# Weights laid out by the host as contiguous 1 MB blocks, 8 KB on each partition

## The chip, the core and the metric

The kernel runs on one core of a Trainium2 chip. The core has TensorE for matrix products, VectorE, ScalarE and GpSimd for elementwise work, and sixteen DMA engines that carry data from memory into the on-chip tiles of 128 partitions. The metric is the device time of one execution in microseconds.

## What is computed

The reference is a stack of two transformer blocks of the usual kind, followed by a third of another kind, on 256 tokens of 1024 features, in 32-bit floats:

```
x: [1, 256, 1024]
for layer in (0, 1):
    h = h + mixer(rmsnorm(h))                # layer 0: gated linear recurrence and forgetting attention
                                             # layer 1: dilated and sliding-window attention
    h = h + cross_attention(rmsnorm(h), mem) # q, k, v, o of 1024 x 1024 each
    h = h + relu(rmsnorm(h) @ w_up) ** 2 @ w_down          # 1024 -> 4096 -> 1024
h = rmsnorm(h)
mod = silu(c) @ w_ada + b_ada                # 1024 -> 6144: shifts, scales and gates
h = h + gt1 * hybrid_mixer(norm(h))          # attention and a gated delta rule, gated together
aff = softmax(h2 @ w_router)                 # 16 experts; each takes its 32 best tokens
y[e] = (silu(xe[e] @ w_gate[e]) * (xe[e] @ w_up[e])) @ w_down[e]     # each matrix 1024 x 1024
h = h + gt2 * (sum of gates * y, put back to the tokens)
```

Each weight is used once. Those of the experts are 3 x 16 x 1024 x 1024 floats, 201 MB of the 394 MB that the kernel reads.

## The kernel before

All weights come from memory in blocks of 1 MB into tiles of 128 partitions x 2048 floats, called `raw` (`fraw` for w_ada). The queue of SyncE issues nearly all of these loads, in the order of their use; a load waits until its tile has been used up by the work before.

The dense products of the first three quarters (`dense_fm_steps` L331, `dense_tm_steps` L353, `mlp` L583) are made with three products of 32-bit halves: `split` (L287) lets ScalarE write the upper part `whi` (L294) and VectorE the lower part `wlo` (L295) of 1024 columns at a time, and `mm3` (L310 to L313) lets TensorE multiply upper by upper, lower by upper and upper by lower. A block of `dense_fm` is 8 chunks of 128 rows by 256 columns of the matrix, so a partition gets 8 pieces of 256 floats (1 KB) from 8 rows; one of `dense_tm` and of the perceptrons' second matrix is 4 chunks by 512 columns (2 KB). `load_chunks` (L269) writes this as a rearranged view of the matrix. The vector `mod` is made beside the perceptrons by VectorE (`modulation`, L957), from blocks of 2 chunks by 1024 columns (4 KB) in tiles `fraw`. At the very start `mixer0` loads its input `xT` and its first weight block in three parts each, as `FIRST` says, so that the first product waits for a part only.

The experts run last. `experts` (L1798) takes them in four groups of 4, `G`. For each group the gate matrices are streamed (`stream`, L1784): for each chunk of 128 input features two blocks, each with 2 experts by 1024 columns (4 KB pieces), and 4 products on each block, in which two experts of 32 tokens stand side by side in the array (L1793). Then the up matrices in the same way, the activation, four transposes for each half, and the down matrices (L1825 to L1845): a block there has 4 experts by 512 columns (2 KB pieces; L1832 loads, L1835 multiplies). In the last group `TAIL` cuts the second half of the columns into two of 256: there a tile holds two chunks with two loads of 512 KB each (1 KB pieces). After a set of columns two products (L1842) put the rows back to their tokens, VectorE adds them to X (L1843), and in the last group the sum is written out (L1845).

Twenty tiles take the blocks of the experts in turn (`raw_tile`, L1773): 8 `early`, which the delta rule's systems use before, 4 `ring`, 5 `ring2` and 3 `ring3`, which come free as the mixer ends. The first blocks are loaded into them while the mixer and the routing still run.

The program's order on each engine is found by a scheduler, which simulates the instructions as they are written.

Of the kernel before, what the change touches and what calls it, by code (L numbers as in the profile page):

```python
# [15 lines left out]
PSUM = bass.MemoryType.PSUM  # L16

P = 128
# [54 lines left out]
def _kchunks(w):  # L73
    import numpy as np

    w = np.asarray(w)
    k, n = w.shape
    return w.reshape(k // P, P, n).transpose(1, 0, 2).reshape(P, -1)

# [131 lines left out]
class Chunks:  # L211
    """Feature chunks kept two to a tile, indexed as one [partition, chunk, token] array."""
# [14 lines left out]
def _body(ctx, tc, I, lay, out, stop):  # L227
# [46 lines left out]
    def wload(src, nk, n):  # L274
        raw = ring.tile([P, 2048], F32, name="raw")
        load_chunks(raw, src, nk)
        return raw

# [27 lines left out]
    def weights(src, nk, n, pre=None, part=1024, slow=()):  # L306
        raw = pre if pre is not None else wload(src, nk, n)
        return split(raw, nk, n, part, slow)
# [22 lines left out]
    def dense_fm_steps(W, c0, ncols, a, emit, kc=8, pre=None, slow=(), first=1024):  # L331
        ah, al = a
        for b0 in range(0, ncols, 256):
            wd = min(256, ncols - b0)
            nb = wd // P
            ws = weights(W[:, c0 + b0:c0 + b0 + wd], kc, wd, pre[b0 // 256] if pre else None, 1024 if b0 else first, slow)
# [16 lines left out]
    def dense_tm_steps(W, c0, ncols, a, emit, kc=8, step=512, part=1024):  # L353
        ah, al = a
        for g0 in range(c0, c0 + ncols, step):
            wd = min(step, c0 + ncols - g0)
            kt = 2048 // step
            ws = [weights(W[k0 * P:(k0 + kt) * P, g0:g0 + wd], kt, wd, part=part) for k0 in range(0, kc, kt)]
# [62 lines left out]
    def transpose_half(gain, j):  # L421
        # features first, for the products that come next: half of the features as soon as they are there
# [30 lines left out]
    def causal_pv(pool, es, v, vcols, o):  # L453
        # two heads at once: their columns of the array are separate
# [19 lines left out]
    def features_first(src, gain, pool, name, raw=None):  # L474
        if raw is None:
            raw = wload(src, 8, S)
# [18 lines left out]
    def mem_k(l, a, kT):  # L495
# [5 lines left out]
        return dense_fm_steps(I["xa_w_kv"][l], 0, D, a, ek)  # L501

    def mem_v(l, a, v):
# [3 lines left out]
        return dense_tm_steps(I["xa_w_kv"][l], D, D, a, ev, step=VS)  # L507

    def cross_attention(l, kT, v, pool):
# [12 lines left out]
        def split_own(x, nm, lo, w):  # L522
# [3 lines left out]
            for c in range(0, 2048, w):  # L526
# [8 lines left out]
               # the lower part of the values takes the place of the keys  # L535
               split_own(v, "vMh", lambda: kvs.tile([P, 2, D], F32R, name=f"kT{l}"), 512)]
        for n, _ in enumerate(dense_fm_steps(I["xa_w_q"][l], 0, D, a, eq)):
# [41 lines left out]
        dense_tm(I["xa_w_o"][l], 0, D, (oh, ol), add_x, gain=pv(f"g_ml{l}"))  # L579

    def mlp(l, pool, side, done):
# [4 lines left out]
        Wu, Wd = I["mlp_w_up"][l], I["mlp_w_down"][l]  # L586
# [26 lines left out]
        for g in range(8):  # L613
# [3 lines left out]
            for n in range(2):  # L617
                ws = weights(Wd[g * 512:(g + 1) * 512, n * 512:(n + 1) * 512], 4, 512)
# [15 lines left out]
    def mixer0(pool):  # L634
        W = I["ab_w_in"][0]
        # the first product waits for a half of its operands only
        xraw, wraw = (ring.tile([P, 2048], F32, name="raw") for _ in range(2))
        for k0, k1 in FIRST:
            load_chunks(xraw, I["xT"], 8, k0, k1)
            load_chunks(wraw, W[:, 0:256], 8, k0, k1)  # L640
        wraw = (wraw, wload(W[:, 256:512], 8, 256))
# [25 lines left out]
        # gated linear recurrence  # L667
# [10 lines left out]
        # forget gates: two copies of the eight rows  # L678
# [112 lines left out]
    def mixer1(pool):  # L791
        groups["k2"] = load_group(pool, "k2")
        W = I["cd_w_in"][0]
# [8 lines left out]
        # chunks: 0-3 qc, 4-7 kc, 8-11 qd, 12 kd, 13 kd with its two heads exchanged  # L802
# [98 lines left out]
    class Fill:  # L901
        # steps of other products, to stand between those of a chain
# [24 lines left out]
    def modulation(pool, units):  # L927
        # rows of silu(c) @ w_ada, 1024 columns to a unit: products by feature on DVE, the sum over the features by
        # TensorE at the end of each unit
        c = pv("c")  # L930
        cs = pool.tile([P, 8], F32, name="cs")
        # a window on these columns that starts at 96 - 32 q has ones in its columns 32 q to 32 q + 31 only
# [8 lines left out]
        def load(b, hf, k, first):  # L941
            raw = (ring if first else pool).tile([P, 2048], F32, name="raw" if first else "fraw")
            load_chunks(raw, I["w_ada_2"][0, k * P:(k + 2) * P, b * 2048 + hf * D:b * 2048 + (hf + 1) * D], 2)
            return raw

        for b, hf, k in [(b, hf, k) for b, hf in units for k in range(0, 8, 2)]:
            raw = load(b, hf, k, (b, hf, k) == (*units[0], 0))
# [1016 lines left out]
```

## Time and profile before

| | us |
|---|---|
| median of three runs | 1639.99 (1638.78 to 1642.88) |
| span of the profiled execution | 1637.7 |
| TensorE busy | 1462.6 (89% of the span) |
| VectorE busy | 871.8 (53%) |
| ScalarE busy | 610.1 (37%) |
| data read from memory | 393.62 MB, 241 GB/s over the span |

The profiled execution's own time is its span, 1637.7 us from the first to the last instruction; the median of the timed runs is 2.3 us above it. Busy time is what an engine's instructions cover, averaged over stages that differ. The DMA share of a stretch is the mean over the sixteen engines, and it goes a little over 1 where records of two transfers overlap. The clock of TensorE has two levels, 1.2 and 2.4 GHz, given as 0.50 and 1.00.

### The profile page before, as it was taken

How to read it: one execution, taken by the hardware profiler on the slowest of the kernel's cores; microseconds unless marked ns; L12 is line 12 of the kernel's file. 1: busy time of each engine (PE TensorE's matmuls, PEld its weight loads, DVE VectorE, ACT ScalarE, POOL GpSimd, SP SyncE). 2: the span in 40 equal slices, each digit the busy share in tenths (PEclk: the TensorE clock that was granted, in tenths of full speed). 3: DMA queues.
4: the chain of work that ended last, by engine and by line, in shares of the span. 5: the costliest groups of instructions: out<-in, count | busy, mean ns of one | idle time of the engine just before them, and what ended most of it. 6: DMA issues, size and time to landing. Idle time of an engine off the chain costs nothing.

```text
span 1637.7 us, 25415 instructions
## 1 busy us (share of the span) xinstructions
PE 1462.6 (89%) x10554; PEld 1076.7 (66%) x10554; DVE 871.8 (53%) x1556; ACT 610.1 (37%) x1005; POOL 98.8 (6%) x97
## 2 busy tenths in 40 slices
PE   8999999999999989999967999999797777777776
PEld 8978898999888788999956888899531111111111
DVE  7775668776666677876578985557521001001001
ACT  6755545444444665544435455425210000000000
POOL 0000200000000020000022512100000000000000
PEclk9989999999999999999988999999797996996996
DMA  8635547885543345976521412448699999999999
GB/s 305 207 105 189 170 129 265 288 298 192 179 145 136 104 155 183 315 277 234 195 85 52 130 53 74 161 159 290 243 403 399 411 403 402 414 408 395 413 406 310
DMA packets 212372, 396.33 MB, mean 242 GB/s; under 512 B 6880, under 2 KB 112352, under 8 KB 212128
## 3 DMA queue, kind: packets, MB, share of 16 engines
q1 hardware_dynamic: 211104, 391.27, 66.6%
q10 hardware_dynamic: 864, 2.64, 0.5%
q8 instruction: 83, 1.36, 0.3%
q0 software_dynamic: 288, 0.79, 0.1%
q14 instruction: 33, 0.27, 0.0%
HBM read 393.62 MB, written 1.05 MB: 241 GB/s over the span
## 4 chain that ended last, share of the span: by engine, by line
PE 63%; DMA 24%; DVE 8%; ACT 2%; issue 1%; SPq 1%; DVEq 0%; ACTq 0%
PE mm L313 13%; PE mm L312 13%; PE mm L311 13%; DMA raw<-in_w_down_dram 9%; DMA raw<-in_w_up_dram 8%; DMA raw<-in_w_gate_dram 5%; PE acc L312 3%; PE acc L313 3%; PE acc L311 3%; DVE wlo L295 2%; PE mm L1793 1%; PE acc L1450 1%; PE acc L1793 1%; DMA fraw<-in_w_ada_dram 1%; PE acc L464 1%
## 5 line engine op out<-in xcount | busy, mean ns | idle before, releaser
L295 DVE TENSOR_TENSOR wlo<-raw,whi 128x1024 fp32r<-128x1024 f32 (+1 forms) x303 | 369.3, 1223 | 179.4 <-ACT whi L294 172.7
L294 ACT CAST whi<-raw 128x1024 fp32r<-128x1024 f32 (+1 forms) x303 | 313.5, 1039 | 347.0 <-PE mm L312 176.5
L311 PE MATMUL mm<-hTh,whi 128*128 128x256 f32 x1096 | 312.7, 289 | 7.5 <-ACT whi L294 5.4
L313 PE MATMUL mm<-hTh,wlo 128*128 128x256 f32 x1096 | 313.4, 288 | 4.8 <-DVE wlo L295 4.8
L312 PE MATMUL mm<-hTl,whi 128*128 128x256 f32 x1096 | 314.3, 289 | 1.9 <-DVE hTl L1086 1.9
L311 PEld LDWEIGHTS mm<-hTh,whi 128*128 128x128 f32 x1096 | 211.2, 194 | 13.0 <-ACT whi L294 5.6
L313 PEld LDWEIGHTS mm<-hTh,wlo 128*128 128x128 f32 x1096 | 211.9, 194 | 8.9 <-DVE wlo L295 7.1
L312 PEld LDWEIGHTS mm<-hTl,whi 128*128 128x128 f32 x1096 | 211.9, 194 | 4.2 <-DVE hTl L1086 2.2
L1793 PE MATMUL mm<-raw,xe 128*32 128x512 f32 x512 | 108.2, 598 | 30.6 <-DMA raw<-in_w_up_dram 30.6
L1793 PE MATMUL acc<-raw,xe 128*32 128x512 f32 x512 | 102.4, 620 | 22.7 <-DMA raw<-in_w_gate_dram 22.7
L1793 PEld LDWEIGHTS mm<-raw,xe 128*32 128x32 f32 x512 | 22.3, 109 | 113.3 <-DMA raw<-in_w_up_dram 74.2
L1811 ACT ACTIVATE sgl<-acc 128x512 f32<-128x512 f32 x8 | 4.7, 597 | 230.1 <-PE acc L1793 230.1
L1793 PEld LDWEIGHTS acc<-raw,xe 128*32 128x32 f32 x512 | 21.6, 112 | 98.7 <-DMA raw<-in_w_gate_dram 57.1
L311 PE MATMUL acc<-whi,hh 128*128 128x512 f32 x192 | 75.0, 391 | 0.0
L312 PE MATMUL acc<-wlo,hh 128*128 128x512 f32 x192 | 74.9, 391 | 0.0
L313 PE MATMUL acc<-whi,hl 128*128 128x512 f32 x192 | 74.2, 390 | 0.0
L1820 DVE SCALAR_TENSOR_TENSOR sgl<-sgl,mm 128x512 f32<-128x512 f32 x8 | 5.4, 686 | 116.3 <-PE mm L1793 116.3
L1835 PE MATMUL acc<-raw,xe 128*32 128x512 f32 x256 | 47.7, 850 | 21.6 <-DMA raw<-in_w_down_dram 21.6
L1835 PE MATMUL mm<-raw,xe 128*32 128x512 f32 (+1 forms) x320 | 43.2, 641 | 26.0 <-DMA raw<-in_w_down_dram 26.0
L957 DVE SCALAR_TENSOR_TENSOR macc<-fraw,cs,macc 128x1024 f32<-128x1024 f32 x40 | 51.2, 1281 | 20.7 <-DMA fraw<-in_w_ada_dram 20.3
L1812 DVE SCALAR_TENSOR_TENSOR sgl<-sgl,acc 128x512 f32<-128x512 f32 x8 | 5.4, 686 | 106.3 <-ACT sgl L1811 106.3
L312 PE MATMUL mm<-wlo,hTh 128*128 128x256 f32 (+2 forms) x192 | 58.7, 307 | 0.3 <-DVE wlo L295 0.3
(525 smaller groups left out, 2618.2 us busy)
## 6 DMA issues: line engine op xcount, KB each, us to landing
raw<-in_w_gate_dram SPq DMA_DIRECT2D x64, 1024.0 KB, 17.8
raw<-in_w_up_dram SPq DMA_DIRECT2D x64, 1024.0 KB, 18.3
raw<-in_w_down_dram SPq DMA_DIRECT2D x56, 1024.0 KB, 14.4
raw<-in_mlp_w_up_dram SPq DMA_DIRECT2D x32, 1024.0 KB, 5.4
raw<-in_mlp_w_down_dram SPq DMA_DIRECT2D x32, 1024.0 KB, 5.4
fraw<-in_w_ada_dram SPq DMA_DIRECT2D x22, 1024.0 KB, 6.7
raw<-in_w_in_dram SPq DMA_DIRECT2D x19, 1024.0 KB, 5.1
raw<-in_xa_w_kv_dram SPq DMA_DIRECT2D x16, 1024.0 KB, 5.5
```

The lines of the kernel that those rows point to most:

```text
L294: nc.scalar.copy(hi[:, a:b], raw[:, c0 + a:c0 + b])
L295: (nc.gpsimd if len(parts) in slow else nc.vector).tensor_sub(lo[:, a:b], raw[:, c0 + a:c0 + b], f(hi[:, a:b]))
L311: mm(o, lh, rh, start=start, stop=False, skip_group_check=True)
L312: mm(o, lh, rl, start=False, stop=False, skip_group_check=True)
L313: mm(o, ll, rh, start=False, stop=stop, skip_group_check=True)
L464: mm(o[j * 64:j * 64 + 64, q0:S], v[:, k, vcol:vcol + 64], pT[:, c0:c0 + S - q0], start=k == 0, stop=k == 1, skip_group_check=True)
L957: nc.vector.scalar_tensor_tensor(acc[:, sl], w, ck, acc[:, sl], OP.mult, OP.add)
L1450: mm(o[J, c], lh[J, c], rh[J, c], start=True, stop=True)
L1793: ins = mm(banks[n][j * 32:(j + 1) * 32, :], xe[:, c, G * P + j * 32:G * P + (j + 1) * 32], raw[:, e * D + n * 512:e * D + (n + 1) * 512], ...
L1812: nc.vector.scalar_tensor_tensor(sg[:, sl], sg[:, sl], 1.0, bg[n], OP.add, OP.mult)
L1820: nc.vector.scalar_tensor_tensor(sg[:, sl], sg[:, sl], 0.5, bu[n], OP.mult, OP.mult)
L1835: mm(by[j * 32:(j + 1) * 32, :], hT[:, c + k, j * 32:(j + 1) * 32], raw[:, k, j, :], start=c + k == 0, stop=c + k == 7, tile_position=(0, ...
```

## The change

The host now lays out every large weight matrix as a list of blocks of 128 x 2048 floats, in the order in which the kernel loads them (`LOADS`, `_laid`; for the experts `_expert_loads`, one array `wx` with gate, up and down of each group in turn). A load takes one block, whose row for each partition is contiguous: 8 KB, or the part of it that a smaller block fills. Inside a tile the data lie as before, so that the splits and products are the same instructions. `xT` and `memT` are laid out by `_kchunks` in the same manner. The two loads of 512 KB into a tile of the narrow columns become one of 1 MB. Constants, gains, `x` and `mem` keep their layout. The core of the diff (the other changed lines are comments taken out and calls that now go through `weight`):

```diff
+LOADS = {
+    "ab_w_in": _fm(0, 2048) + _tm(2048, 512, 512),
...
+    "mlp_w_up": _fm(0, 4 * D),
+    "mlp_w_down": [(g * 512, 4, n * 512, 512) for g in range(8) for n in range(2)],
+    "w_ada_2": [(k * P, 2, b * D, D) for b in range(6) for k in range(0, 8, 2)],
...
+def _laid(w, loads):
...
+    out = np.zeros((w.shape[0], len(loads), P, 2048), w.dtype)
+    for i, (r, nk, c, n) in enumerate(loads):
+        out[:, i, :, :nk * n] = (w[:, r:r + nk * P, c:c + n].reshape(-1, nk, P, n).transpose(0, 2, 1, 3)
+                                 .reshape(-1, P, nk * n))
+    return out.reshape(-1, 2048)
+
+def _expert_loads(g, u, d):
...
+    for G in range(4):
+        es = slice(G * 4, G * 4 + 4)
+        for w in (g, u):
+            out.append(w[es].reshape(2, 2, 8, P, D).transpose(2, 0, 3, 1, 4).reshape(-1, 2048))
+        for c0, w in _tail(G):
+            kn = 512 // w
+            out.append(d[es, :, c0:c0 + w].reshape(4, 8 // kn, kn, P, w).transpose(1, 3, 2, 0, 4).reshape(-1, 2048))
+    return np.concatenate(out)
...
-    def load_chunks(raw, src, nk, k0=0, k1=None):
-        n = src.shape[1]
-        v = raw[:, :nk * n].rearrange("p (k c) -> p k c", k=nk)
-        nc.sync.dma_start(v[:, k0:k1, :], src.rearrange("(k p) c -> p k c", p=P)[:, k0:k1, :])
...
+    def load(raw, src, k0=0, k1=None, n=256):
+        w = src.shape[1] if k1 is None else k1 * n
+        nc.sync.dma_start(raw[:, k0 * n:w], src[:, k0 * n:w])
...
+    def raw_next():
+        raw, i = raw_tile(), (n_raw[0] - 1) * P
+        nc.sync.dma_start(raw, I["wx"][i:i + P, :])
+        return raw
...
-            raw = raw_tile()
-            e0 = G * 4 + pr * 2
-            nc.sync.dma_start(raw.rearrange("p (e n) -> p e n", e=2),
-                              W[e0:e0 + 2, c * P:(c + 1) * P, :].rearrange("e p n -> p e n"))
+            raw = raw_next()
...
-                    raw = raw_tile().rearrange("p (k e n) -> p k e n", k=kn, e=4)
-                    for k in range(kn):
-                        nc.sync.dma_start(raw[:, k, :, :], Wd[G * 4:G * 4 + 4, (c + k) * P:(c + k + 1) * P, sl].rearrange("e p n -> p e n"))
+                    raw = raw_next().rearrange("p (k e n) -> p k e n", k=kn, e=4)
```

The order of the instructions is the same on VectorE, ScalarE and GpSimd. On SyncE each load stands where it stood; only its form changes. At the program's start, where `xT` is the transposed input and `ab_w_in` the first matrix, before:

```order
L272 DMA raw<-in_xT_dram 128x2x256
L272 DMA raw<-in_ab_w_in_dram 128x2x256
L272 DMA raw<-in_xT_dram 128x2x256
L272 DMA raw<-in_ab_w_in_dram 128x2x256
L272 DMA raw<-in_xT_dram 128x4x256
L272 DMA raw<-in_ab_w_in_dram 128x4x256
L272 DMA raw_104<-in_ab_w_in_dram 128x8x256
```

and after:

```order
L341 DMA raw<-in_xT_dram 128x512
L341 DMA raw<-in_ab_w_in_dram 128x512
L341 DMA raw<-in_xT_dram 128x512
L341 DMA raw<-in_ab_w_in_dram 128x512
L341 DMA raw<-in_xT_dram 128x1024
L341 DMA raw<-in_ab_w_in_dram 128x1024
L341 DMA raw_104<-in_ab_w_in_dram 128x2048
```

The three parts of each block are kept; a partition's two, four and eight pieces of 256 floats are one piece now. On SyncE at the end of the last group of experts, before (raw_13782 is the last block of 512 columns, those after it have 256):

```order
L1832 DMA raw_13782<-in_w_down_dram 128x4x512
L1832 DMA raw_13798<-in_w_down_dram 128x4x256 x2
L1832 DMA raw_13809<-in_w_down_dram 128x4x256 x2
L1832 DMA raw_13820<-in_w_down_dram 128x4x256 x2
L1832 DMA raw_13831<-in_w_down_dram 128x4x256 x2
L1832 DMA raw<-in_w_down_dram 128x4x256 x8
L1845 DMA out_dram<-X 128x512 x2
L1845 DMA out_dram<-X 128x256 x4
```

and after:

```order
L1860 DMA raw_13782<-in_wx_dram 128x2048
L1860 DMA raw_13798<-in_wx_dram 128x2048
L1860 DMA raw_13808<-in_wx_dram 128x2048
L1860 DMA raw_13818<-in_wx_dram 128x2048
L1860 DMA raw_13828<-in_wx_dram 128x2048
L1860 DMA raw<-in_wx_dram 128x2048 x4
L1918 DMA out_dram<-X 128x512 x2
L1918 DMA out_dram<-X 128x256 x4
```

Sixteen loads have become eight. On TensorE at the same place, where `acc` and `mm` are the sums of the first 512 and the next 256 columns, `xe` the hidden features, and `tp<-sgl,modR` the product that puts rows back to their tokens, before:

```order
L1835 MATMUL acc<-raw_13782,xe 32x512 x4
L1835 MATMUL mm<-raw_13798,xe 32x256 x4
L1842 MATMUL tp<-sgl,modR 128x512 x2
L1835 MATMUL mm<-raw_13798,xe 32x256 x4
L1835 MATMUL mm<-raw_13809,xe 32x256 x8
L1835 MATMUL mm<-raw_13820,xe 32x256 x8
```

and after:

```order
L1908 MATMUL acc<-raw_13782,xe 32x512 x4
L1915 MATMUL tp<-sgl,modR 128x512 x2
L1908 MATMUL mm<-raw_13798,xe 32x256 x8
L1908 MATMUL mm<-raw_13808,xe 32x256 x8
L1908 MATMUL mm<-raw_13818,xe 32x256 x8
```

The two products that put the first 512 columns back have moved ahead of the four products on the first half of the next block; the same happens nowhere else.

## Rows read from the trace of the kernel before

**Rows 1.** The page's forty slices: busy tenths, DMA share and rate of each.

```profile
PE   8999999999999989999967999999797777777776
DMA  8635547885543345976521412448699999999999
GB/s 305 207 105 189 170 129 265 288 298 192 179 145 136 104 155 183 315 277 234 195 85 52 130 53 74 161 159 290 243 403 399 411 403 402 414 408 395 413 406 310
```

**Rows 2.** Stretches: bounds, length, busy us (instructions) by engine, clock, DMA share, GB/s.

```profile
300.00:400.00 100.00, 100.00 (x632) 91.00 (x631) 74.57 (x74) 48.62 (x57) 1.04 (x2) 1.00 0.78 265
1180.00:1631.00 451.00, 339.35 (x1715) 80.32 (x1715) 37.06 (x73) 15.20 (x32) 0.00 (x0) 0.88 1.03 402
```

**Rows 3.** TensorE's waits, 12 to 1174 us, then 1226 to 1632: total, times, longest.

```profile
PE mm L313 <- DVE wlo L295: 4.8, 8, 1.1
...
PE mm L1793 <- DMA raw<-in_w_up_dram: 30.6, 48, 1.0
PE mm L1835 <- DMA raw<-in_w_down_dram: 26.0, 24, 2.1
PE acc L1793 <- DMA raw<-in_w_gate_dram: 22.7, 37, 0.7
PE acc L1835 <- DMA raw<-in_w_down_dram: 21.6, 21, 1.7
```

**Rows 4.** DMA issues: count, size of each, median us to landing.

```profile
raw<-in_w_gate_dram SPq DMA_DIRECT2D x64, 1024.0 KB, 17.8
raw<-in_w_up_dram SPq DMA_DIRECT2D x64, 1024.0 KB, 18.3
raw<-in_w_down_dram SPq DMA_DIRECT2D x56, 1024.0 KB, 14.4
...
raw<-in_w_down_dram SPq DMA_DIRECT2D x16, 512.0 KB, 9.6
```

**Rows 5.** The chain that ended last, at the first expert products: start, us, what.

```profile
1174.63 3.60 PE acc L1793 x16
```

**Rows 6.** Stretches with one size of piece: 4 KB twice, 2 KB, 1 KB.

```profile
1380.00:1450.00 70.00, 54.25 (x226) 11.40 (x228) 3.51 (x5) 1.19 (x2) 0.00 (x0) 0.95 1.02 412
1540.00:1560.00 20.00, 15.18 (x64) 2.91 (x63) 1.38 (x2) 1.19 (x2) 0.00 (x0) 1.00 1.02 410
1215.00:1245.00 30.00, 24.43 (x154) 8.04 (x148) 4.96 (x11) 3.34 (x6) 0.00 (x0) 0.89 1.05 386
1612.00:1622.00 10.00, 5.24 (x58) 1.36 (x56) 1.85 (x3) 0.00 (x0) 0.00 (x0) 0.82 1.08 346
```

**Rows 7.** The load of k2: ScalarE's queue, its landing, two stretches while it flows.

```profile
439.34 0.34 ACTq L241 DMA_DIRECT2D k<-in_k_dram  x1
...
441.00:443.00 2.00, 2.00 (x19) 2.00 (x18) 1.15 (x5) 1.64 (x4) 0.00 (x0) 1.00 0.95 381
441.50:443.00 1.50, 1.50 (x15) 1.50 (x14) 0.91 (x5) 1.14 (x3) 0.00 (x0) 1.00 0.99 421
```

**Rows 8.** Instructions in order of time on TensorE, and the clock of a stretch.

```profile
1550.13 1.91 PE L1793 MATMUL mm<-raw,xe 128*32 128x512 f32 x8 [0.65 <-DMA raw<-in_w_up_dram]
...
1601.80 1.94 PE L1835 MATMUL acc<-raw,xe 128*32 128x512 f32 x8 [0.68 <-DMA raw<-in_w_down_dram]
...
1599.00:1611.00 12.00, 9.53 (x41) 1.71 (x42) 0.75 (x1) 0.00 (x0) 0.00 (x0) 0.50 1.07 369
```

**Rows 9.** The line that issues gate and up loads: ns minimum, median, maximum.

```profile
L1788 SPq DMA_DIRECT2D raw<-in_w_gate_dram x64: 367/2108/4716, 1035.0 to 1526.7; - x64
```

**Rows 10.** The start: instructions in order of time; waits of ScalarE and VectorE for loads.

```profile
14.74 0.39 PE L313 MATMUL mm<-hTh,wlo 128*128 128x256 f32 x1 [0.30 <-DVE wlo L295]
...
ACT whi L294 <- DMA raw<-in_ab_w_in_dram: 2.8, 3, 1.3
...
DVE macc L957 <- DMA fraw<-in_w_ada_dram: 20.3, 12, 3.1
```

**Rows 11.** The end on TensorE, in order of time: the last landing.

```profile
1631.20 0.64 PE L1835 MATMUL mm<-raw,xe 128*32 128x256 f32 x8 [0.69 <-DMA raw<-in_w_down_dram]
```

More of the change, by code (lines that the diff above doesn't have):

```diff
@@ L78, in _kchunks, with _fm, _tm, _tail @@
     return w.reshape(k // P, P, n).transpose(1, 0, 2).reshape(P, -1)
+def _fm(c0, n, kc=8):
+    return [(0, kc, c0 + b, min(256, n - b)) for b in range(0, n, 256)]
+def _tm(c0, n, step, kc=8):
+    kt = 2048 // step
+    return [(k * P, kt, g, min(step, c0 + n - g)) for g in range(c0, c0 + n, step) for k in range(0, kc, kt)]
+LOADS = {
+    "ab_w_in": _fm(0, 2048) + _tm(2048, 512, 512),
+    "ab_w_out": _tm(0, D, 512),
+    "cd_w_in": _fm(0, 1024) + _tm(1024, 512, 512) + _fm(1536, 512) + _fm(2048, 128) + _tm(2176, 128, 512),
+    "cd_w_out": _tm(0, D, 512),
+    "xa_w_q": _fm(0, D),
+    "xa_w_kv": _fm(0, D) + _tm(D, D, VS),
+    "xa_w_o": _tm(0, D, 512),
+    "mlp_w_up": _fm(0, 4 * D),
+    "mlp_w_down": [(g * 512, 4, n * 512, 512) for g in range(8) for n in range(2)],
+    "w_ada_2": [(k * P, 2, b * D, D) for b in range(6) for k in range(0, 8, 2)],
+    "w_in_2": _tm(0, 768, 256) + _fm(768, 1536) + _tm(2304, 512, 256) + _fm(2848, 2048),
+    "w_attn_up_2": _fm(0, D, 4),
+    "w_dn_up_2": _fm(0, D, 4),
+    "w_o_2": _tm(0, D, 256),
+}
+def _laid(w, loads):
+    import numpy as np
+    out = np.zeros((w.shape[0], len(loads), P, 2048), w.dtype)
[4 more added lines that the diff above has]
+def _expert_loads(g, u, d):
+    import numpy as np
+    out = []
+    for G in range(4):
[6 more added lines that the diff above has]
+    return np.concatenate(out)
+def _tail(G):
+    return TAIL if G == 3 else ((0, 512), (512, 512))
+class Weight:
+    def __init__(self, ap, loads, layer):
+        self.ap, self.at = ap, {(r, c): layer * len(loads) + i for i, (r, _, c, _) in enumerate(loads)}
+    def load(self, r, nk, c, n):
+        i = self.at[r, c] * P
+        return self.ap[i:i + P, :nk * n]
 def _block_diag(w):
@@ L335, in dense_fm_steps @@
             nb = wd // P
-            ws = weights(W[:, c0 + b0:c0 + b0 + wd], kc, wd, pre[b0 // 256] if pre else None, 1024 if b0 else first, slow)
+            ws = weights(None if pre else W.load(0, kc, c0 + b0, wd), kc, wd, pre[b0 // 256] if pre else None, 1024 if b0 else first, slow)
             ps = bank_mm()
@@ L357, in dense_tm_steps @@
             kt = 2048 // step
-            ws = [weights(W[k0 * P:(k0 + kt) * P, g0:g0 + wd], kt, wd, part=part) for k0 in range(0, kc, kt)]
+            ws = [weights(W.load(k0 * P, kt, g0, wd), kt, wd, part=part) for k0 in range(0, kc, kt)]
             if step == 256:
@@ L1654, in eo @@
             nc.vector.scalar_tensor_tensor(sl, sl, back[:, t:t + 1], ps, OP.mult, OP.add)
-        for n, _ in enumerate(dense_tm_steps(I["w_o_2"][0], 0, D, a, eo, step=256)):
+        for n, _ in enumerate(dense_tm_steps(weight("w_o_2"), 0, D, a, eo, step=256)):
             if n % 8 == 2 and n > 8:
@@ L1856, in _body @@
         fill.pull(FE)
-        dense_tm(I["ab_w_out"][0], 0, D, y, add_x, gain=pv("g_xa0"))
+        dense_tm(weight("ab_w_out"), 0, D, y, add_x, gain=pv("g_xa0"))
     if stop == "mix0":
@@ L1872, in _body @@
         fill.pull()
-        dense_tm(I["cd_w_out"][0], 0, D, y, add_x, gain=pv("g_xa1"))
+        dense_tm(weight("cd_w_out"), 0, D, y, add_x, gain=pv("g_xa1"))
     if stop == "mix1":
@@ L1938, in _arrays @@
     a = {k: np.ascontiguousarray(v) for k, v in inputs.items()}
-    arrays = {k: a[k] for k in _W}
-    arrays["xT"] = np.ascontiguousarray(a["x"][0].T)
-    arrays["memT"] = np.ascontiguousarray(a["mem"][0].T)
+    arrays = {k: a[k] for k in ("x", "mem")}
+    arrays.update({k: _laid(a[k], loads) for k, loads in LOADS.items()})
+    arrays["wx"] = _expert_loads(*(a[k][0] for k in ("w_gate_2", "w_up_2", "w_down_2")))
+    arrays["xT"] = _kchunks(a["x"][0].T)
+    arrays["memT"] = _kchunks(a["mem"][0].T)
     groups = dict(_params(a))
```

58 lines of the change are left out of this document (29 added, 29 removed).

## The prediction, made before the changed kernel ran

> **What bounds the kernel now.** I read the page first, in forty slices [rows 1]. TensorE is at nine tenths or more in most of the first 29 slices, while the DMA engines lie anywhere between one and nine tenths and move 52 to 317 GB/s. From the thirtieth slice on the picture turns over: the DMA line shows nine tenths in every slice, the rate is flat near 405 GB/s until the last, and TensorE drops to seven or so. The change touches both parts, so each needs its own price.
>
> The stretch views give these parts in numbers [rows 2]. In a multilayer-perceptron stretch (300 to 400 us) TensorE is busy for 100 of 100 us and the DMA engines for 78%. In the expert stretch (1180 to 1631 us) the sixteen DMA engines are busy for 1.03 of the time (records overlap a little) and TensorE for 339 of 451 us. The list of TensorE's waits says the same [rows 3]: between 1226 and 1632 us it waits for loads of the three expert matrices, 30.6 + 26.0 + 22.7 + 21.6 = 100.9 us; between 12 and 1174 us no load stands among its releasers at all, only the other engines (the row shown is the one that comes back below). So the first 1178 us end when TensorE ends, and the last 450 when the DMA engines end.
>
> How much is loaded in the last part? The experts need 64 + 64 + 56 + 8 = 192 blocks of 1 MB (the 16 issues of 512 KB are 8 blocks) [rows 4]. Twenty tiles hold them (8 early, 4 ring, 5 and 3 more), and they are full before the first product: it starts at 1174.63 [rows 5]. That leaves 172 blocks for the stretch. The check is in [rows 2]: 402 GB/s for 451 us is 181.3 MB; less about 0.8 MB of the output, 180.5 MB are 172.1 blocks of 1.0486 MB.
>
> **The expert stretch, the main term.** Before, a partition's row of a block is cut into pieces: gate and up 2 pieces of 4 KB, down 4 pieces of 2 KB, the narrow last columns of down 8 pieces of 1 KB. After, it is always one piece of 8 KB. The trace has a stretch of each [rows 6]: 410 GB/s for 4 KB pieces, 386 for 2 KB, 346 for 1 KB (with some output beside it), all with the engines full. Per block that is 2.558, 2.717 and 3.031 us. An engine serves 8 partitions of a block, so it handles 16, 32 and 64 pieces. From 16 to 32 pieces the block costs 0.159 us more, 9.9 ns a piece; from 32 to 64 it costs 0.314 us more, 9.8 ns a piece. The two agree: each piece has a fixed cost of about 9.9 ns beside its bytes. With 8 pieces a block should take 2.558 - 8 x 0.0099 = 2.479 us, or 423 GB/s. That is an extrapolation, but the trace has one load with 8 KB rows, the 1 MB of constants k2 that ScalarE's queue issues at 439.34: once it flows, 421 GB/s at a DMA share of 0.99 [rows 7], 2.491 us a block.
>
> The sum for the stretch: 172 x 2.479 = 426.4 us, plus 1.9 us for the 0.8 MB of output, 428.3, against 451: 22.7 us less. The same sum for before (108 blocks of gate and up at 2.558, 56 of down at 2.717, 8 at 3.031, plus 1.9) gives 454.6, 0.8% above the 451 of the trace, because the rates are a little better in places than in the steady stretches. Scaled alike, the difference is 26.1 us. With the measured 421 and no scaling it is 451 - 430.4 = 20.6 us. I take **24 us less**, between the two ways of counting, and keep 20.6 and 26.1 as ends.
>
> Here a rule of the Trainium skill speaks against the change. The row first: the engines are full at 346, 386 and 410 GB/s with three sizes of piece [rows 6], so size matters well above 1 KB. The page "DMA: Bandwidth & Descriptors", section Specifications, names 512 B as the smallest transfer that reaches line rate, and no piece of the experts was smaller. By that rule the sum would be nothing; by the rows it is 24 us, and the rows decide.
>
> **Does the rest keep up?** TensorE must take a block in 2.48 us where it now has 2.56 to 2.72. At a granted clock of 1.00 (2.4 GHz; the stretch from 1540 in [rows 6]) the eight products of a lone up block fill 1.91 us, and 0.65 us of waiting go before them [rows 8]. At 0.50 (1.2 GHz, from 1599 to 1611) a down block takes 1.94 us [rows 8], and two gate blocks worked together at the stage's start take 3.60 us [rows 5]. All lie under 2.48 a block, so TensorE still waits for the loads, even at its lower level. SyncE's issue instruction has a median of 2108 ns, near the time of a block, but a minimum of 367 [rows 9]: it fills the time until the queue takes more, and the engines are never short of work. Issues fall by 8 only (the pairs of 512 KB become one). I cost issue at nothing; if it were itself the limit, the DMA share would be under 1.
>
> **The first 1178 us.** Every load here also has larger pieces, but the work that hides them is TensorE's, and it is full. What can be gained is what is waited for. At the start ScalarE waits 2.8 us for the first matrix in three places, and the product behind the last of them, at 14.74, had 0.30 us of idle time [rows 10]. With 1 KB pieces becoming 2, 4 and 8 KB the 3 MB ahead land about 3 x 0.5 us sooner, of which TensorE can use its short gaps: 0.7 us, between 0 and 1.5. In the perceptrons VectorE waits 20.3 us for the blocks of w_ada, and all that reaches TensorE by way of VectorE's lower halves is 4.8 us in eight places [rows 3, 10]. Those blocks gain 2.558 - 2.479 = 0.08 us each and a little from shorter queues: I take 0.3 us, between 0 and 4.8. The first prefetches of the experts land sooner too, which is worth nothing: the tiles are full and the queue stands still until routing is done.
>
> **The tail.** The last eight blocks, four for each 256 columns, came as two halves of 512 KB; now each lands as one. Before, eight products of 0.64 us follow the last landing [rows 11]. Afterwards sixteen wait for it: 0.64 us **more**, between 0 and 1.3 (at the lower clock). The only shift in the order is next to it: the pair of products that adds the preceding columns to X now stands ahead of a block's eight, not between four and four. It costs nothing where TensorE waits for loads anyway.
>
> Sum: -24.0 - 0.7 - 0.3 + 0.6 = **-24.4 us**. Profiled span 1637.7, so 1613.3; the median of the runs, 1639.99, lies 2.3 above that span, which I carry over: 1615.6. All ends together give 1609 (26.1, 1.5, some 4 us in the perceptrons, tail as above) and 1621 (20.6, nothing, nothing, 1.3).
>
> **Rivals.**
>
> *A ceiling near 412 GB/s that pieces do not set.* If the memory or the ports give no more than the better 4 KB stretches do (412 between 1380 and 1450 [rows 6]), then only the 2 KB and 1 KB pieces gain: 172 x 2.545 + 1.9 = 439.6, 11.4 us less, in all 1628. For it: 412 is flat over many slices. Against it: the 421 of k2, and that the fixed cost per piece came out equal twice. Chance 12%. The same page of the Trainium skill, section Where 436 GB/s comes from, puts the memory's limit for one core at about 358 GB/s; the trace, at 410, has already passed it.
>
> *Size of a piece does not matter, or the new layout is not what moves.* Then the 386 of the 2 KB stretch is a matter of the matrix down, of its place in memory, and nothing changes: 1639 to 1640. Against it: three sizes on one line. Chance 4%. The rule on 512 B above would give this.
>
> *Slower: the sixteen engines disturb each other in memory.* With rows of 8 KB laid end to end, all engines read at equal distances in one block, in step. If that costs rate for good, the whole stretch pays. The point from which it decides is the present mean: below 402 GB/s the kernel is slower. The price: k2 with its start included moved 381 GB/s [rows 7]; at 381 the stretch takes 172 x 2.752 + 1.9 = 475 us, 24 more, in all 1664. For it: 1.5 us of k2 is a short witness, and its first microsecond was slow. Against it: the start of any single load is slow, and the flowing part is the fastest rate among these rows. Chance 5%.
>
> *More than the sum: the perceptron and projection parts gain too,* because shorter loads free VectorE and the tiles sooner: all of the 4.8 us and some idle time elsewhere, below 1609. Chance 5%, as TensorE is at 100 of 100 us there.
>
> **How the numbers follow.** The forecast has 74% and its time, 1615.6. With the ceiling (12%) the range from 1609 to 1628 holds 86%; without the ceiling's end it would hold less than 8 in 10. About 0.3%, 5 us, is what a measurement of this kernel can tell from no change. Faster than that: 74 + 12 + 5 = 91%. Within: 4%. Slower: 5%.
>
> **What the changed profile should show.** The forty slices: the last ten or eleven near 423 GB/s, the early ones with the same TensorE digits and lower DMA digits. The number of pieces falls: the page's DMA packets should be a quarter or so of those of before. The first product of the experts still starts near 1174, within 2 us; from there to the last landing 24 us less. TensorE's waits for the expert loads fall from 100.9 us to about 77, since its work is the same. A gate stretch and a down stretch have the same rate. Wrong would be: 410 in all stretches (the ceiling), a rate under 402 (disturbance), a DMA share below 1 in the expert stretch (something other than the engines has become the limit), or a first product much earlier than 1172 (the TensorE part gained).

## The result and the profile after

The changed kernel takes 1617.16 us in the median of four runs (1616.3 to 1620.21); the kernel before, on the same chip, 1641.43 us (1638.78 to 1643.16). The ratio is 0.9866 with an interval of 0.9846 to 0.9885: 22.0 us less, between 18.9 and 25.3. The forecast was 1615.6 in a range of 1609 to 1628. The profiled execution is the longest of the four (1620.21, span 1618.4), so its trace shows a few us less of the gain than the median does.

The page of the changed kernel: the span, the forty slices of [rows 1], the DMA packets, and the loads of the experts and of w_up of the perceptron (KB each, median us from issue to landing).

```profile
span 1618.4 us, 25406 instructions
...
PE   8999999999999999999968899999797776876776
...
DMA  8535437776543343886532311436789999999998
GB/s 309 209 105 182 165 131 256 287 299 211 196 143 118 118 156 133 324 294 244 185 111 79 105 54 54 156 133 234 312 327 422 424 424 424 423 422 423 423 424 356
...
DMA packets 58004, 396.33 MB, mean 245 GB/s; under 512 B 6752, under 2 KB 7776, under 8 KB 11424
...
raw<-in_wx_dram SPq DMA_DIRECT2D x192, 1024.0 KB, 19.7
...
raw<-in_mlp_w_up_dram SPq DMA_DIRECT2D x32, 1024.0 KB, 4.9
```

The picture is that of [rows 1], with nine of the last ten slices flat at 422 to 424 GB/s where they wandered between 395 and 414; the last slice holds the end of the program. In the earlier slices TensorE's digits are nearly the same. The packets fall from 212372 to 58004, the quarter or so that was foretold.

Stretches of the changed kernel (bounds, length, busy us and instructions of PE, PEld, DVE, ACT and POOL, clock, DMA share, GB/s): the answers to [rows 2] and to the 2 KB and 4 KB stretches of [rows 6].

```profile
300.00:400.00 100.00, 100.00 (x632) 90.98 (x631) 74.60 (x74) 48.52 (x57) 1.04 (x2) 1.00 0.73 264
1180.00:1612.00 432.00, 330.38 (x1721) 79.48 (x1717) 37.80 (x74) 15.89 (x34) 0.00 (x0) 0.92 1.01 420
...
1215.00:1245.00 30.00, 25.52 (x181) 9.14 (x180) 5.13 (x13) 3.99 (x8) 0.00 (x0) 0.94 1.01 422
1540.00:1560.00 20.00, 15.28 (x64) 3.02 (x64) 0.00 (x0) 0.00 (x0) 0.00 (x0) 1.00 1.01 423
```

The perceptron stretch has the same 100 us of TensorE in 100, and 264 GB/s against 265; only the share of time in which the DMA engines are busy fell, from 0.78 to 0.73. The whole gain lies in the expert stretch, where the engines are as full as before (1.01) and move 420 GB/s for 402, and where a load of down now runs at the rate of gate and up.

The two ends of that stretch, in order of time (start, us, what, idle time before it): TensorE's first expert products, and its last two landings.

```profile
1176.60 3.66 PE L1869 MATMUL acc<-raw,xe 128*32 128x512 f32 x16
...
1609.58 1.07 PE L1908 MATMUL mm<-raw,xe 128*32 128x256 f32 x16 [1.00 <-DMA raw<-in_wx_dram]
1611.99 1.07 PE L1908 MATMUL mm<-raw,xe 128*32 128x256 f32 x16 [1.35 <-DMA raw<-in_wx_dram]
```

From the first product to the last landing it is 1611.99 - 1176.60 = 435.4 us. By [rows 5, 11] it was 1631.20 - 1174.6 = 456.6 us. That is **21.2 us less**. I call this the length of the expert stretch below. The first product itself comes 2.0 us later; over all runs its time shows no tie to the layout of the loads (last section).

### The profile page after: what moved, and what is told of

It is laid out like the page before. It is cut to its first block, busy times and chain, and to the rows that moved or that the text cites. A ratio compares the mean times of both kernels' runs of the same rounds, so it can differ in the third digit from the quotient of the medians.

```text
span 1618.4 us, 25406 instructions
## 1 busy us (share of the span) xinstructions
PE 1453.3 (90%) x10554; PEld 1075.5 (66%) x10554; DVE 870.8 (54%) x1556; ACT 610.3 (38%) x1005; POOL 99.7 (6%) x97
## 2 busy tenths in 40 slices
DMA packets 58004, 396.33 MB, mean 245 GB/s; under 512 B 6752, under 2 KB 7776, under 8 KB 11424
## 4 chain that ended last, share of the span: by engine, by line
PE 63%; DMA 25%; DVE 7%; ACT 3%; issue 1%; POOL 1%; SPq 0%; DVEq 0%; ACTq 0%
DMA raw<-in_wx_dram 24%; PE mm L385 14%; PE mm L384 14%; PE mm L383 14%; PE acc L384 3%; PE acc L385 3%; PE acc L383 3%; PE acc L1524 2%; DVE wlo L367 1%; PE acc L1869 1%; PE acc L536 1%; DVE raw L1132 1%; PE mm L917 1%; ACT whi L366 1%; DMA fraw<-in_w_ada_dram 1%
## 5 line engine op out<-in xcount | busy, mean ns | idle before, releaser
L1031 DVE SCALAR_TENSOR_TENSOR macc<-fraw,cs,macc 128x1024 f32<-128x1024 f32 x40 | 51.2, 1281 | 18.1 <-DMA fraw<-in_w_ada_dram 17.8
L385 PE MATMUL mm<-whi,hTl 128*128 128x256 f32 (+2 forms) x192 | 58.8, 307 | 0.0
```

Source lines behind the costliest of these rows:

```text
L385: mm(o, ll, rh, start=False, stop=stop, skip_group_check=True)
L1031: nc.vector.scalar_tensor_tensor(acc[:, sl], w, ck, acc[:, sl], OP.mult, OP.add)
```

## Experiments: where the gain comes from

**e1_experts_only** is the kernel before with the new layout for the three expert matrices alone; **e2_dense_only** is the changed kernel with those three as they were. The core of e1's edit against the kernel before (e2's against the changed kernel is its reverse):

```diff
-            nc.sync.dma_start(raw.rearrange("p (e n) -> p e n", e=2),
-                              W[e0:e0 + 2, c * P:(c + 1) * P, :].rearrange("e p n -> p e n"))
+            raw = raw_next()
```

> Only the experts' three matrices are laid out as blocks of 8 KB rows; all other weights as before. Theory (a fixed cost for each piece, paid where the DMA engines are the limit): nearly the whole gain, 24 us, so about 1617, with the rate near 423 GB/s from the first expert product to the last landing and TensorE's part unchanged. Rival (a good part of the gain comes from the first 1178 us, through earlier landings): at least 5 us of the 24 are missing, 1622 or more.

> All weights but the experts' are laid out as blocks; the experts' loads stay as before. Theory: within 2 us of the kernel before, 1639 to 1642, since TensorE waits for no load there; the expert stretch at 386 and 410 GB/s as before. Rival (the earlier part gains too): 1635 or less.

Measured: e1 1620.43 us (1616.16 to 1621.34), ratio 0.9883, interval 0.9863 to 0.9903; e2 1639.78 us, ratio 0.9996, interval 0.9981 to 1.001; before 1640.11. The same window of all four kernels, 1210 to 1590 us, in the order before, changed, e1, e2:

```profile
1210.00:1590.00 380.00, 285.21 (x1312) 61.36 (x1304) 24.04 (x40) 11.08 (x20) 0.00 (x0) 0.89 1.03 405
```
```profile
1210.00:1590.00 380.00, 286.69 (x1376) 61.61 (x1376) 24.23 (x42) 11.73 (x22) 0.00 (x0) 0.92 1.01 423
```
```profile
1210.00:1590.00 380.00, 282.18 (x1376) 60.83 (x1368) 24.20 (x42) 11.74 (x22) 0.00 (x0) 0.94 1.01 423
```
```profile
1210.00:1590.00 380.00, 284.88 (x1322) 61.65 (x1314) 23.01 (x41) 10.57 (x20) 0.00 (x0) 0.89 1.03 405
```

The experts' layout alone gives 423 GB/s and a stretch of 435.9 us, everything the change gives; e1's median lies between the theory's 1617 and the rival's 1622, so it is the stretch that decides. The layout of all other weights gives 405 GB/s, 455.4 us, and no difference that can be measured. So the first 1178 us, with 14 matrices laid out anew, earned nothing: TensorE ends last there.

## Experiments: is it the size of a piece?

The new layout changes three things at once: the pieces are longer, a block's addresses lie next to each other, and the blocks lie in the order of their loads. **e3, e4 and e5** keep the last two and cut each 8 KB row back into 2, 4 and 8 pieces, which the host lays out so that a block is still one megabyte without gaps.

```diff
-        nc.sync.dma_start(raw, I["wx"][i:i + P, :])
+        nc.sync.dma_start(raw.rearrange("p (k n) -> p k n", k=2), I["wx"][i:i + 2 * P, :].rearrange("(k p) n -> p k n", p=P))
...
```

> As the changed kernel, and each block of the experts still 1 MB of adjacent addresses in memory, but written as two halves, so that a partition's row comes in two pieces of 4 KB. Theory (fixed cost of 9.9 ns for each piece): all expert loads at 410 GB/s, 172 x 0.079 = 13.6 us more than the changed kernel, about 1631. Rival (it is the adjacent addresses that pay, not the size of the piece): 423 GB/s and 1617 as in the changed kernel.

> As the changed kernel, every block of the experts still 1 MB of adjacent addresses, written so that a partition's row comes in four pieces of 2 KB. Theory (fixed cost for each piece, 7.9 to 9.9 ns by the runs so far): 386 to 393 GB/s in all expert loads, 172 x (0.19 to 0.24) = 33 to 41 us more than the changed kernel, 1650 to 1658, slower than the kernel before, which has pieces of 4 KB for two matrices of three. Rival (the adjacent addresses pay): 1617.

> As the changed kernel, adjacent blocks written so that a partition's row comes in eight pieces of 1 KB. Theory: 340 to 357 GB/s in all expert loads, 172 x (0.46 to 0.58) = 79 to 100 us more than the changed kernel, 1696 to 1717. Rival (the adjacent addresses pay, and the slow 346 of the narrow columns was the output's doing): 1617, or well under 1690.

The same window of e3, e4 and e5:

```profile
1210.00:1590.00 380.00, 283.06 (x1332) 60.61 (x1324) 24.04 (x40) 11.10 (x20) 0.00 (x0) 0.92 1.02 413
```
```profile
1210.00:1590.00 380.00, 278.94 (x1280) 59.85 (x1272) 22.84 (x40) 10.56 (x20) 0.00 (x0) 0.88 1.05 392
```
```profile
1210.00:1590.00 380.00, 257.02 (x1144) 54.23 (x1136) 21.29 (x36) 8.72 (x16) 0.00 (x0) 0.85 1.09 356
```

| pieces of | whole time, us | expert stretch, us | GB/s, 1210 to 1590 | us for a block |
|---|---|---|---|---|
| 1 KB (e5) | 1696.07 | 513.8 | 356 | 2.945 |
| 2 KB (e4) | 1655.85 | 468.0 | 392 | 2.675 |
| 4 KB (e3) | 1628.60 | 444.1 | 413 | 2.539 |
| 8 KB (changed) | 1617.16 | 435.4 | 423 | 2.479 |

(The last column is 1.0486 MB by the rate. e3, e4 and e5, like e6, e7, e10 and e11 below, are single runs, while thirteen runs of the kernel before on e3's chip lie between 1634.85 and 1644.31; so the stretch and the rate carry the argument, and not the whole time.) With everything else as in the changed kernel, the size of the pieces alone makes the kernel faster or slower than before. From 1 KB to 2 KB an engine handles 32 pieces fewer in a block and saves 0.270 us, 8.4 ns each; then 16 fewer save 0.136 us, 8.5 ns each; then 8 fewer save 0.060 us, 7.5 ns each. That is the fixed cost per piece that the prediction rests on; its 9.9 ns were a fifth to a third too much. With them e3 was priced too high as well: 13.6 us were foretold, and its stretch is 8.7 us longer than the changed kernel's. e4 and e5 came inside their ranges. Addresses that lie next to each other don't help by themselves: at the same size of piece the kernel before, without them, moved 410 GB/s with 4 KB and 386 with 2 KB [rows 6], and e3 and e4, with them, move 409 and 387 in like stretches (below).

The Trainium skill, page "DMA: Bandwidth & Descriptors", section Specifications, gives 512 B as the smallest transfer at line rate. With all sixteen engines full, 1 KB pieces move 356 GB/s and 8 KB pieces 423, so for a stretch like this the measurement decides against it.

## Experiments: place in memory

**e6_pitch_1536k** and **e7_pitch_2048k** load the same 8 KB pieces, but the blocks lie beside each other instead of behind each other, so that the 128 rows of one block are 192 x 8 KB = 1.5 MB apart, or 2 MB with 64 empty blocks added. This is a strong form of the rival on memory: pieces at equal, large distances.

```diff
-        nc.sync.dma_start(raw, I["wx"][i:i + P, :])
+        nc.sync.dma_start(raw, I["wx"][:, i:i + 2048])
...
```

> As the changed kernel with pieces of 8 KB, but a partition's pieces of all 192 blocks stand in one row of 1.5 MB, so that the 128 pieces of a load start 1.5 MB apart. Theory (only the size of the piece counts): 423 GB/s and 1615 to 1619. Rival (the engines disturb each other where their rows lie far apart at one pitch): a rate under 415 and more than 1625.

> As the run before, with the rows filled up to 2 MB, so that the 128 pieces of a load start at a pitch that is a power of two. Theory (only the size of the piece counts): 423 GB/s and 1615 to 1619. Rival (pieces at such a pitch meet in the same part of memory): below 402 GB/s and slower than the kernel before, over 1640. The Trainium skill, page DMA: Bandwidth & Descriptors, section Latency and other measured facts, gives 164 GB/s for copies with rows of 16 KB at a pitch of 2 MB; by that figure the 172 blocks would take, as an estimate, 1100 us and the kernel about 2290 us.

Measured: e6 1616.58 us, e7 1875.8 us, before on that chip 1643.93. The window of e6 and of e7:

```profile
1210.00:1590.00 380.00, 284.26 (x1364) 60.50 (x1356) 24.04 (x40) 11.08 (x20) 0.00 (x0) 0.93 1.01 423
```
```profile
1210.00:1590.00 380.00, 221.72 (x878) 44.67 (x880) 15.82 (x30) 8.20 (x16) 0.00 (x0) 0.78 1.00 265
```

A distance of 1.5 MB costs nothing that can be seen, one of 2 MB takes 37% of the rate (265 for 423), and there e7's theory, that only the size of the piece counts, is wrong. So contiguous blocks are not what makes the load fast, and a loss of the kind that the forecast's slower rival feared exists on this chip: it came at 2 MB between rows, not at 8 KB and not at 1.5 MB. That it comes from engines that disturb each other is not shown. The DMA share is 1.00 in e7: the engines look full while each piece takes longer, so a full DMA line alone doesn't say that the rate is the best one. The Trainium skill, page "DMA: Bandwidth & Descriptors", section Latency and other measured facts, reports the loss at a 2 MB row pitch, with 164 GB/s for copies in memory with 16 KB rows; for these loads with 8 KB pieces it was 265.

## Experiments: further along the same line, and who pays for a piece

**e9_pieces_16k** loads two blocks with one transfer, 16 KB on a partition, into pairs of tiles; 76 transfers are of that size, 40 blocks of the four tiles of the pool `ring` stay at 8 KB. **e9_again** is the same kernel on another chip, **changed_again** the changed kernel beside it.

```diff
-RING2 = 5
-RING3 = 3
+RING2 = 4
+RING3 = 4
...
+        half[0] = pool.tile([P, 4096], F32, name=name)
+        nc.sync.dma_start(half[0], I["wx"][n * P:(n + 2) * P, :].rearrange("(p a) n -> p (a n)", a=2))
```

> As the changed kernel, but 16 of the 20 expert tiles are taken in pairs, each pair loaded by one transfer of 2 MB with pieces of 16 KB. Theory (fixed cost for each piece): 4 pieces a block instead of 8 save 4 x 9.9 ns; for 0.8 of 172 blocks that is 5.4 us, at about 430 GB/s in those loads; up to 2.5 us are given back where TensorE waits for the second block of a pair. About 1612 to 1615. Rival (a ceiling near 424 GB/s that the pieces no longer set): the rate stays at 424, and the time is that of the changed kernel or up to 3 us above it.

> The kernel with pairs of blocks in pieces of 16 KB once more, beside the changed kernel. Theory (8 ns for each piece): its expert stretch is 5 to 6 us shorter than the changed kernel's, at 428 to 430 GB/s, and the whole 4 to 6 us shorter. Rival (a ceiling, or what the pairs save is given back elsewhere): within 2 us of the changed kernel.

> The changed kernel once more, so that it and the run before stand on the same chip. Theory and rival: 20 to 25 us below the kernel before; its expert stretch 435 to 437 us from the first expert product to the last, against 455 to 457.

| | whole time, us | ratio, interval | expert stretch, us |
|---|---|---|---|
| e9_pieces_16k | 1615.89 (1613.91 to 1616.48) | 0.9858, 0.9839 to 0.9878 | 429.6 |
| e9_again | 1614.86 (1610.81 to 1617.4) | 0.9848, 0.9827 to 0.9868 | 428.5 |
| changed_again | 1620.61 (1613.78 to 1622.44) | 0.9876, 0.9854 to 0.9898 | 434.7 |

The window of e9_again and of changed_again:

```profile
1210.00:1590.00 380.00, 241.82 (x1384) 56.77 (x1376) 25.01 (x42) 10.89 (x21) 0.00 (x0) 0.85 1.01 428
```
```profile
1210.00:1590.00 380.00, 288.76 (x1384) 62.37 (x1376) 24.20 (x42) 11.74 (x22) 0.00 (x0) 0.92 1.01 423
```

The stretch is shorter by 5.8 and 6.2 us, close to the 5.4 foretold, and the fewer pieces go on paying; e9 also needs 76 transfers fewer, and no run separates the two. In the whole time the medians on one chip are 5.8 us apart, but the intervals overlap, so this version is the best measured here without being clearly separated from the changed kernel.

**e10_1k_two_queues** is e5 with every second block issued on ScalarE's queue. If the fixed cost were a matter of one queue that takes its pieces one by one, a second queue would hide a part of it.

```diff
-        nc.sync.dma_start(raw.rearrange("p (k n) -> p k n", k=8), I["wx"][i:i + 8 * P, :].rearrange("(k p) n -> p k n", p=P))
+        (nc.scalar if n_raw[0] % 2 else nc.sync).dma_start(raw.rearrange("p (k n) -> p k n", k=8), I["wx"][i:i + 8 * P, :].rearrange("(k p) n -> p k n", p=P))
...
```

> The experts' blocks in pieces of 1 KB, as in the earlier run, but every second block is issued by ScalarE's queue in place of SyncE's. Theory (the fixed cost of a piece is paid in the sixteen engines, which serve both queues): the rate stays at 356 GB/s or a little below. Rival (it is paid in a queue, and the other queue's pieces fill the gap): over 375 GB/s and over 20 us less than with one queue, 1675 or below.

```profile
1210.00:1590.00 380.00, 202.90 (x1202) 57.48 (x1200) 22.28 (x40) 8.96 (x18) 0.00 (x0) 0.81 1.09 358
```

358 GB/s against 356, the share of the engines at 1.09 in both: the cost stays, so it is not the queue's. The whole time, 1703.78, is longer than e5's 1696.07; ScalarE, which now issues loads, has its own work later, and TensorE waits 103.3 us in three places for its xe.

## Experiment: the start

The first product of TensorE came later, not sooner (below). The theory was that the small load of p0, which ScalarE's queue issues, shares the engines with the now larger pieces of SyncE's and lands later. **e11_gains_first** issues it on SyncE's queue, ahead of the others.

```diff
-    groups["p0"] = load_group(cons, "p0")
+    groups["p0"] = load_group(cons, "p0", nc.sync)
```

> As the changed kernel, but the small load of gains that the first work of ScalarE waits for (52 KB, 416 bytes a partition) is the first in SyncE's queue instead of alone in ScalarE's. Theory (in the changed kernel it shares the engines with larger pieces and lands 0.9 us later): it lands before 3 us, and the first product of TensorE starts near 5.4 us instead of 6.1, with no change of the whole time beyond 0.5 us. Rival (the first product waits for its weights): 6 us or later.

The small load did land early, 1.7 us after its issue for 3.6 in the changed kernel and 2.5 before, but the first product did not come earlier. Here are ScalarE's first conversion and TensorE's first product, in order of time: first the changed kernel, then ScalarE's row of e11.

```profile
4.41 0.91 ACT L554 ACTIVATE hTh<-raw,p 128x256 fp32r<-128x256 f32 x2 [1.75 <-DMA p<-in_p_dram]
...
6.09 0.58 PE L383 MATMUL mm<-hTh,whi 128*128 128x256 f32 x1 [6.09 <-ACT whi L366]
```
```profile
4.69 0.91 ACT L554 ACTIVATE hTh<-raw,p 128x256 fp32r<-128x256 f32 x2 [2.47 <-DMA raw<-in_xT_dram]
```

In the changed kernel ScalarE waits for p, as the theory says; with p first it waits for the inputs that now stand behind p, until 4.69, and the first product comes at 6.19 us instead of 6.09. The whole time of e11 (1626.15) says nothing about the start: its first expert product is at 1184.0, and TensorE's order differs from that of the changed kernel from about 850 us on, in the third block's mixer, because the scheduler orders the work anew when the load is moved. Its expert stretch is 433.7 us.

## Why the prediction was right, and where its terms were off

**What bounds the kernel: right.** TensorE up to 1178 us, the DMA engines after. e1 and e2 show it from both sides.

**The main term, 24 us: it measured 21.2.** The mechanism is the one foretold, a fixed cost per piece. What failed is the size of this cost: 9.9 ns were put on every block, where the windows above give 7.5 to 8.5 on average. So the sum for before (454.6 us) came out above the trace (451); both sums were scaled alike to 26.1, and 24 lay in the middle; the end of 20.6, by the flowing rate of k2 [rows 7], was nearly exact. The reason shows when the window is cut finer. Two stretches each of e5, e4, e3 and the changed kernel:

```profile
1336.00:1376.00 40.00, 24.63 (x116) 5.02 (x120) 1.38 (x2) 1.17 (x2) 0.00 (x0) 0.86 1.10 348
1322.00:1332.00 10.00, 6.76 (x30) 1.51 (x32) 0.00 (x0) 0.00 (x0) 0.00 (x0) 1.00 1.09 386
```
```profile
1326.00:1360.00 34.00, 22.13 (x110) 4.76 (x112) 1.38 (x2) 1.17 (x2) 0.00 (x0) 0.94 1.05 387
1314.00:1322.00 8.00, 5.88 (x26) 1.27 (x28) 0.00 (x0) 0.00 (x0) 0.00 (x0) 1.00 1.05 409
```
```profile
1320.00:1342.00 22.00, 15.57 (x82) 3.57 (x80) 1.37 (x2) 1.17 (x2) 0.00 (x0) 1.00 1.02 409
1301.00:1312.00 11.00, 8.76 (x40) 1.74 (x36) 0.00 (x0) 0.00 (x0) 0.00 (x0) 1.00 1.03 422
```
```profile
1320.00:1347.00 27.00, 19.93 (x100) 4.00 (x96) 1.37 (x2) 1.17 (x2) 0.00 (x0) 0.89 1.01 421
1304.00:1314.00 10.00, 7.91 (x34) 1.51 (x32) 0.00 (x0) 0.00 (x0) 0.00 (x0) 1.00 1.01 426
```

And two of the kernel before, with 4 KB pieces:

```profile
1400.00:1410.00 10.00, 7.45 (x32) 1.51 (x32) 0.00 (x0) 0.00 (x0) 0.00 (x0) 1.00 1.03 410
1412.00:1420.00 8.00, 6.38 (x28) 1.13 (x24) 0.00 (x0) 0.00 (x0) 0.00 (x0) 1.00 1.02 420
```

Each of these kernels has two levels, and in e3, e4 and e5 the faster one comes back once in a turn of the twenty tiles, for about four blocks (in e4 at about 1314 and again at 1367, a turn of 53 us). In the slower level the blocks take 3.013, 2.709, 2.564 and 2.491 us: 9.5, 9.1 and 9.1 ns per piece, close to the 9.9 of the prediction, whose rows of 386 and 410 GB/s [rows 6] are all of this level. In the faster one they take 2.717, 2.564, 2.485 and 2.461: 4.8, 4.9 and 3.0 ns per piece. So a fifth of the blocks had less to gain. The 8 KB rate over the whole window, 423 foretold, is 423, but partly by luck: the forecast went out from the slower level, which moves 421 with 8 KB pieces, and the faster blocks lift the mean. Redone with both levels, 16 tiles to 4, and 1.9 us of output as in the prediction: a gate or up block took 0.8 x 2.558 + 0.2 x 2.485 = 2.543 us before, a down block 0.8 x 2.717 + 0.2 x 2.564 = 2.686, a block now 0.8 x 2.491 + 0.2 x 2.461 = 2.485. The sum for before is 108 x 2.543 + 56 x 2.686 + 8 x 3.031 + 1.9 = 451.2 us, which is the 451 of [rows 2]; for after it is 172 x 2.485 + 1.9 = 429.3. The difference, 21.9, is within 1 us of the measured 21.2; the same difference between e2 and e1 is 455.4 - 435.9 = 19.5, so one pair of traces fixes it to some 2 us only. The 0.8% that the prediction's sum was too high was the sign of a second level; scaling hid it.

**TensorE keeps up: right, but its waits fell less than foretold**, from 100.9 us [rows 3] to 89.4, not to 77. The waits of the changed kernel's TensorE from 1226 to 1612 us (total, times, longest), and the two groups of its instructions there that became cheaper (busy us, mean ns, idle time before):

```profile
PE mm L1869 <- DMA raw<-in_wx_dram: 28.6, 48, 2.0
PE acc L1869 <- DMA raw<-in_wx_dram: 23.0, 41, 0.7
PE acc L1908 <- DMA raw<-in_wx_dram: 19.2, 21, 1.5
PE mm L1908 <- DMA raw<-in_wx_dram: 18.6, 19, 1.5
...
L1908 PE MATMUL acc<-raw,xe 128*32 128x512 f32 x256 | 43.4, 779 | 19.2 <-DMA raw<-in_wx_dram 19.2
...
L1915 PE MATMUL tp<-sgl,modR 128*128 128x512 f32 (+1 forms) x32 | 19.3, 738 | 6.8 <-DVE sgl L1911 6.8
```

In the kernel before, these two groups were 47.7 and 25.3 us, at means of 850 and 939 ns:

```profile
L1835 PE MATMUL acc<-raw,xe 128*32 128x512 f32 x256 | 47.7, 850 | 21.6 <-DMA raw<-in_w_down_dram 21.6
...
L1842 PE MATMUL tp<-sgl,modR 128*128 128x512 f32 (+1 forms) x32 | 25.3, 939 | 5.9 <-DVE sgl L1838 5.9
```

The work is the same, but the granted clock over the expert stretch is 0.92 where it was 0.88 [rows 2]: less of it fell into time at 1.2 GHz. "Its work is the same" was right for the instructions and wrong for their time. TensorE isn't the bound here, so nothing of the total hangs on it.

**SyncE's issue at nothing: right.** The issue of a gate block took a median of 2108 ns before [rows 9]; that of an expert block now:

```profile
L1860 SPq DMA_DIRECT2D raw<-in_wx_dram x192: 327/328/1009, 1037.2 to 1592.4; - x192
```

An instruction that became 6 times shorter changed nothing, since the DMA share was 1.03 before and is 1.01 now.

**The start, -0.7 us: wrong, about 0.** The first product of TensorE moved from 5.42 to 6.09 us, mainly because ScalarE's first conversion waits for p until 4.41 where it began at 3.96 before. Later loads are sooner (ScalarE's wait ahead of 12.20 us is 0.99, the row of before at 12.38 had 1.33), and by 10.6 us the two kernels are 0.1 us apart. The step that failed: the prediction priced the three large loads and not the small one that runs beside them on another queue. Why it lands later is not shown; e11 moved it and only moved the wait.

**The perceptrons, -0.3 us: about 0.** TensorE's waits for VectorE's lower halves are 4.5 us (4.8 in [rows 3]), and VectorE's waits for w_ada 17.8 us (20.3 in [rows 10]); e2, with all of that in it, is at 0.9996.

**The tail, +0.6 us: about 0.** Sixteen products follow the last landing where eight did, 1.07 us for 0.64, as foretold (in the trace's count, two records for each product of the program). But from that landing to the end of the span it is 1618.4 - 1611.99 = 6.4 us, and 1637.7 - 1631.20 = 6.5 us before.

**The sum.** The stretch gives -21.2 and the other terms nothing that the traces show. The medians are 24.3 us apart (1641.43 and 1617.16), the ratio's interval is 18.9 to 25.3 us, and it holds the 21.2 as well; on the chip of changed_again the medians are 20.3 us apart (1640.94 and 1620.61). That the forecast of -24.4 came so near to the medians is partly luck: its terms add up to some 3 us more than the traces show.

**The rivals.** The ceiling near 412 GB/s falls with 423, and again with 428 in e9. That size doesn't matter falls with e3 to e5. That the engines disturb each other in memory falls for this layout with 423 too; e7 shows a layout that does lose rate. The gain elsewhere falls with e2.

## What to carry to other kernels

Look first for the stretch in which the DMA line is full: only there did the layout of the weights pay here. There, count the pieces that a block falls into on one engine; each cost 7.5 to 8.5 ns here on average beside its bytes, so that 8 or 16 KB on a partition are worth having, while contiguous blocks as such are worth nothing and rows 2 MB apart are dear. And when a sum built from steady rows misses the measured stretch by even 1%, look for the second level instead of scaling.

## What the runs showed that was not expected

**Four of the twenty tiles load faster.** At 1 KB pieces the faster level is 386 GB/s for 348. In e5 a block arrives at TensorE every 3.0 us, then five times every 2.6 to 2.9 (start, us, what, idle time before):

```profile
1317.04 1.91 PE L1869 MATMUL mm<-raw,xe 128*32 128x512 f32 x8 [1.09 <-DMA raw<-in_wx_dram]
1320.06 1.91 PE L1869 MATMUL mm<-raw,xe 128*32 128x512 f32 x8 [1.11 <-DMA raw<-in_wx_dram]
1322.93 1.91 PE L1869 MATMUL mm<-raw,xe 128*32 128x512 f32 x8 [0.96 <-DMA raw<-in_wx_dram]
1325.48 1.91 PE L1869 MATMUL mm<-raw,xe 128*32 128x512 f32 x8 [0.65 <-DMA raw<-in_wx_dram]
```

Counted in turns of twenty from the first block, the faster ones are about the ninth to the twelfth, which are the tiles of the pool `ring`. The DMA records of e5 show it piece by piece: between 1200 and 1590 us a 1 KB piece takes 46.3 ns on its engine on average into a tile of `ring` and 51.1 into any other. In the programs of all these kernels those four tiles start at multiples of 256 bytes within a partition, and the other sixteen 64 bytes beyond one. Whether that is the cause, or something else in which this pool differs, no run here shows: a kernel with the other sixteen moved by 192 bytes was not tried. The offset alone is not enough: before the stretch, while the tiles are first filled, the median piece of e5 takes 46 ns into both kinds. If it is, the changed kernel would gain 16/20 x 172 x (2.491 - 2.461) = some 4 us more, an estimate from the two levels above, and the kernel before some 13 without any new layout (by 0.8 x 108 blocks of 0.073 us and 0.8 x 56 of 0.153). The Trainium skill, page "DMA: Bandwidth & Descriptors", section How a descriptor splits into AXI transactions, says that the first access of a descriptor which doesn't start on a multiple of 256 B begins at the multiple below it, and that the bytes ahead of the start are fetched unused and still cost beats of the transfer. It says so of reading; here it is the address written that is off, so the rows agree in direction and no more.

**TensorE's part isn't the same length twice.** In the mixer near 900 us only the form of the loads was changed, and TensorE waits for no load there, yet the changed kernel falls back by 2 us. One stretch, before and then after:

```profile
830.00:970.00 140.00, 110.63 (x1214) 97.30 (x1213) 121.38 (x268) 62.98 (x118) 45.94 (x45) 0.88 0.25 76
```
```profile
830.00:970.00 140.00, 110.98 (x1194) 97.56 (x1193) 118.44 (x264) 61.95 (x117) 46.81 (x45) 0.85 0.23 76
```

The granted clock is 0.88 and 0.85: TensorE, which idles for a fifth of this stretch, is granted 1.2 GHz for parts of it that differ from one execution to the next: changed_again, the same program as the changed kernel, has 0.87 there and its first expert product at 1178.1 instead of 1176.6. e1, whose loads up to there are those of the kernel before, has it at 1176.9. Leaving out e11, the first expert product lies between 1173.6 and 1178.3 us over all the runs here, whatever the layout. For an effect of a few us the length of the stretch is therefore a better measure than the time of the whole.
